# Queries, keys and score maxima as float16 pairs with a power-of-two scale, in a two-layer encoder of gated mixing and attention

## The chip, the core and the metric

The kernel runs on one core of a Trainium2 chip. Its engines work side by side, each through its own queue of instructions in order: TensorE (PE in the profile; its weight loads are PEld), VectorE (DVE), ScalarE (ACT), GpSimd (POOL) and SyncE (SP), which here issues all the transfers. TensorE writes to the eight banks of PSUM; everything else lies in SBUF or, in between, in DRAM. The metric is the device time of one execution in microseconds (us), lower is better.

## The reference

The input x is 2048 tokens by 1024 channels. Each of two layers does:

```python
h    = rmsnorm(x, pre_g[l])
proj = h @ w_in[l]                       # 1024 -> 2816 columns
u_a, v_a, g_a, q, k, v, g_b = split(proj)
y_a  = gmlp_group(u_a, v_a, ...) * silu(g_a)
y_b  = gqa_axial_attention(q, k, v, q_norm_g[l], k_norm_g[l], tables) * silu(g_b)
x    = x + rmsnorm(concat(y_a, y_b) @ w_out[l], post_g[l])
```

and the attention, with 8 query heads on 2 key heads of 64 channels, all tokens seeing all tokens:

```python
q = rope(rmsnorm(q, qn_g)); k = rope(rmsnorm(k, kn_g))
sc = einsum('bqkgd,bskd->bkgqs', qblk, k) * 64 ** -0.5
p  = softmax(sc)
o  = einsum('bkgqs,bskd->bqkgd', p, v)
```

Each head of q and k is normalised over its 64 channels and multiplied by a gain vector (`q_norm_g`, `k_norm_g`); in the inputs here these gains are about 8.

## The kernel before, in words

**Number format.** Products run on TensorE in a 32-bit format of reduced precision (F32R in the code, f32 in the profile). To keep accuracy, an operand is split in a high part (the value rounded to F32R) and a low part (the rest), and a product is made of two or three products of parts. Probabilities and values are pairs of float16.

**A layer has two stages.** In the projection stage (0 to 629 us and 1390 to 2019 us of the profile) the tokens go through in four groups of 512 (`GRP`), two at a time. `hT` holds the normalised, transposed tokens of a group, and every column block of `w_in` is loaded, split (`split_w`, lines 252 and 253) and multiplied. A list of small delayed jobs (`Background`, `bg.add(delay, f)`) is worked off between the products, two at most per `tick`: transposes, splits and stores go in there. With them, towards the end of the stage, goes the search for score maxima of the first eight units (`before`, called from `run`).

**Keys.** `do_kv` takes the projected keys of a group through `norm_rope` (lines 333 to 348) and writes, for each tile of 128 tokens and both key heads, a tile `kk` with three parts side by side: the high part (line 371, ScalarE), a second copy of it (372, ScalarE), and the low part (373, GpSimd). The delayed job `trans` transposes high and copy together, and the low part alone, four transposes a tile; line 380 (ScalarE) copies the first to `k_st`, whose 128 partitions hold the high part twice, and line 382 (VectorE) the other to the lower 64 partitions of `k_lo`. Row 64 of `k_lo` is a row of ones, written by a transfer from `ones1` once a layer (line 1167).

**Queries.** `do_q` does the same with a group's queries; its `trans` transposes first, then splits: line 397 (ScalarE) makes the high part `fh`, line 398 (VectorE) the low part `fl`, and four transfers put them into the DRAM tensor `q_d`.

**Attention.** A unit is one query block of 512 with one head: 32 units a layer, each with 16 key tiles. A unit needs a maximum for each query: `load_qm` brings its queries (high and low, 128 partitions) to `q_m`, 16 steps `max_step` multiply them with 512 keys at a time (`pmax`) and reduce on VectorE (`mx`), `max_row` negates, and `stack_max` transposes, adds the constant EXP_SHIFT on ScalarE (line 683) and stores the row into `m_d`. `load_q` brings `q_st` (high and low) and `q2` (the high part, and the maximum's row as row 64).

The order in the main loop of `attend` is written by hand: `PE`, `ACT`, `DVE` and `POOL` are engines wrapped so that their instructions keep program order, and in the profile all of these have line 84. For key tile k it issues: the two products `sp` (high keys with high and low queries; low keys and the row of ones with high queries and maxima), two exponentials from `sp`, one to the float16 `p_hi` (`p_parts<-sp`) and one to the 32-bit `p_f`, and a subtraction that makes the low part `p_lo`, on GpSimd or, for 15 tiles in 100, on VectorE. Then come jobs due at this step (`at`), a share of the output projection (`pout`, from the list `fill`), and the product of values with `p_hi` of three tiles ago (`LAG`). At every eighth tile a batch follows: the products of `p_lo` of eight tiles and the sums, 64 products with 32 columns of weights each (`po`, `sums`). `finish` divides by the sums and gates. Seven PSUM banks are shared by `sp`, `pmax`, `po`, `pout` and the small tiles.

**Memory.** `big` is a pool of seven buffers of 16 KB a partition for `hT`, `k_st`, `k_lo`, `v_st` and the split `w_out` (`wo`). `fp` has ten buffers of 2 KB for the small tiles.

**Gains.** `gains` loads both gain vectors, once in order and once with their halves swapped, and multiplies that of the queries by 64 ** -0.5 (line 198, VectorE). `rope_rows` multiplies the rotary table by them on GpSimd (line 325).

Of the kernel before, what the change touches and what calls it, by code (L numbers as in the profile page):

```python
# [19 lines left out]
P = 128  # L20
# [4 lines left out]
NH = 8  # L25
# [13 lines left out]
def encoder(ctx: ExitStack, tc, x, w_in, w_out, pre_g, post_g, ln_a_g, ln_a_b,  # L39
# [10 lines left out]
    big = ctx.enter_context(tc.tile_pool(name="big", bufs=7))  # L50
# [8 lines left out]
    def big_t(shape, name):  # L59
        return big.tile(shape, F32R, name=name, tag="big")  # L60
# [114 lines left out]
    class Project:  # L175
# [184 lines left out]
        def do_kv(self, g, banks):  # L360
# [6 lines left out]
            for i, kr in enumerate(krs):  # L367
                for j in range(2):
                    t = g * TPG + 2 * i + j
# [5 lines left out]
                    def trans(t=t, kk=kk):  # L375
# [4 lines left out]
                        nc.scalar.copy(k_st[:, :, t * P:(t + 1) * P],  # L380
                                       pk[:, 0:2 * P].rearrange("p (k s) -> p k s", k=NKV))
                        nc.vector.tensor_copy(k_lo[0:HD, :, t * P:(t + 1) * P],
                                              pk[0:HD, 2 * P:4 * P].rearrange("p (k s) -> p k s", k=NKV))
                    bg.add(KK_DELAY + 2 * (2 * i + j), trans)

        def do_q(self, g, banks, b):
            qrs = self.norm_rope([ps.rearrange("p (t h d) -> p t h d", t=2, d=HD) for ps in banks], 4,
                                 self.rope_rows(g, self.gain_q))
            for i, qr in enumerate(qrs):
                def trans(i=i, qr=qr):  # L390
# [7 lines left out]
                    nc.vector.tensor_tensor(lo, ps, hi.bitcast(F32), ALU.subtract)  # L398
                    for a, part in enumerate((hi, lo)):
                        for h in range(2):  # L400
                            dst = q_d[g][4 * b + h:4 * b + 4:2, a, :, i * 2 * P:(i + 1) * 2 * P]
                            nc.sync.dma_start(dst.rearrange("k d t -> d k t"),
                                              part.bitcast(F32)[h * HD:(h + 1) * HD])
# [212 lines left out]
    def attend(l, kv, nxt):  # L616
# [31 lines left out]
        def load_qm(u):  # L648
            qb, h = units[u]
            s = state[u]  # L650
            s.qm = f_t("q_m", dt=F32R)
            nc.sync.dma_start(s.qm.bitcast(F32), q_d[qb][h].rearrange("a d t -> (a d) t"))
            s.mx = small.tile([P, TPG, NG], F32, name="mx", bufs=3)

        def load_q(u):
            qb, h = units[u]
            s = state[u]
            s.qs = f_t("q_st", dt=F32R)
            nc.sync.dma_start(s.qs.bitcast(F32), q_d[qb][h].rearrange("a d t -> (a d) t"))
            s.q2 = f_t("q2", dt=F32R)  # L660
            nc.sync.dma_start(s.q2.bitcast(F32)[0:HD], q_d[qb][h, 0])
            nc.sync.dma_start(s.q2.bitcast(F32)[HD:HD + 1], m_d[qb][h:h + 1])
# [14 lines left out]
        def stack_max(u, pe, act):  # L677
# [4 lines left out]
            rows = small.tile([TPG, P], F32R, name="m_rows")  # L682
            act.activation(rows, ps[0:TPG, 0:P], AF.Copy, bias=EXP_SHIFT)
            nc.sync.dma_start(m_d[qb][h].rearrange("(t p) -> t p", p=P), rows.bitcast(F32))
# [388 lines left out]
        for k in range(end + 4):  # L1073
            if k < total:
# [9 lines left out]
                ACT.activation(p_hi(k), sp, AF.Exp)  # L1084
                ACT.activation(p_f(k), sp, AF.Exp)
# [76 lines left out]
    for l in range(DEPTH):  # L1162
        kv = [big_t([P, NKV, S], "k_st"), big_t([P, NKV, S], "k_lo")]
# [3 lines left out]
        nc.sync.dma_start(kv[1].bitcast(F32)[HD:HD + 1].rearrange("p k (n i) -> p (k n) i", i=P),  # L1167
                          ones1.unsqueeze(1).broadcast_to([1, NKV * S // P, P]))
# [44 lines left out]
```

## Time and profile before

| | us |
|---|---|
| median of 3 runs | 2810.36 (2807.75 to 2815.12) |
| the profiled execution | 2813.78 |
| its span | 2812.0 |
| projection stage of layer 1 and 2 | 628.9, 628.8 |
| attention stage of layer 1 and 2 | 761.0, 756.8 |
| mean granted TensorE clock | 0.993 |

The stages are bounded here by the first `sp` product or exponential and the last one. Busy time is the union of an engine's instructions; on TensorE and ScalarE an instruction's recorded time overlaps that of the next, so that the pace of a chain of instructions is read from the starts, and the time of one is longer than its step. A row of the groups reads: line, engine, operation, output<-inputs, shapes, count, busy us, mean ns of one, idle us of the engine just before, and what ended that idleness. A row of the windows reads: stretch, its length, then busy us and count for PE, PEld, DVE, ACT and POOL, the granted clock, the share of the transfer engines and GB/s. A row of the chain reads: start, length, engine and tile.

### The profile page before, as it was taken

How to read it: one execution, taken by the hardware profiler on the slowest of the kernel's cores; microseconds unless marked ns; L12 is line 12 of the kernel's file. 1: busy time of each engine (PE TensorE's matmuls, PEld its weight loads, DVE VectorE, ACT ScalarE, POOL GpSimd, SP SyncE). 2: the span in 40 equal slices, each digit the busy share in tenths (PEclk: the TensorE clock that was granted, in tenths of full speed). 3: DMA queues.
4: the chain of work that ended last, by engine and by line, in shares of the span. 5: the costliest groups of instructions: out<-in, count | busy, mean ns of one | idle time of the engine just before them, and what ended most of it. 6: DMA issues, size and time to landing. Idle time of an engine off the chain costs nothing.

```text
span 2812.0 us, 49354 instructions
## 1 busy us (share of the span) xinstructions
PE 2738.1 (97%) x18294; PEld 2067.2 (74%) x18294; DVE 1894.9 (67%) x3976; ACT 1583.3 (56%) x3295; POOL 1300.1 (46%) x1112
## 2 busy tenths in 40 slices
PE   7999999999999999999999999999999999999997
PEld 7998899885556666566699989998755666666665
DVE  7863788876666666666497639798766555656654
ACT  5322432228887777777642225322478877777774
POOL 1210121018776676666532111200377766767665
PEclk9999999999999999999999999999999999999999
DMA  4533433422222232232345343342322232221323
GB/s 134 165 110 108 137 108 90 124 90 97 85 85 89 94 91 97 87 100 89 139 151 151 122 128 121 102 124 91 112 68 94 78 100 71 83 92 59 115 71 127
DMA packets 276563, 293.71 MB, mean 104 GB/s; under 512 B 20450, under 2 KB 214306, under 8 KB 276324
## 3 DMA queue, kind: packets, MB, share of 16 engines
q1 hardware_dynamic: 276324, 290.57, 33.1%
q8 instruction: 145, 2.38, 0.3%
q14 instruction: 94, 0.77, 0.1%
HBM read 197.02 MB, written 93.45 MB: 103 GB/s over the span
## 4 chain that ended last, share of the span: by engine, by line
PE 79%; DVE 12%; ACT 4%; issue 2%; DMA 1%; POOL 1%; SPq 0%; DVEq 0%; POOLq 0%; ACTq 0%
PE pp L84 25%; PE sp L84 16%; PE pout L84 12%; PE po L84 12%; PE pmax L84 7%; PE sums L84 4%; PE pt L84 2%; DVE fc L346 2%; DVE w_lo L253 2%; ACT p_parts L84 1%; ACT p_f L84 1%; DMA w_raw<-in_w_in_dram 1%; DVE mx L670 1%; DVE o_t L84 1%; DVE fb L435 1%
## 5 line engine op out<-in xcount | busy, mean ns | idle before, releaser
L84 POOL TENSOR_TENSOR p_parts<-p_f,p_parts 128x512 f16<-128x512 f32 x872 | 1038.7, 1207 | 438.9 <-ACT p_f L84 256.7
L84 ACT ACTIVATE p_parts<-sp 128x512 f16<-128x512 f32 x1024 | 627.6, 613 | 334.5 <-PE sp L84 323.1
L84 DVE TENSOR_REDUCE mx<-pmax 128x1 f32<-128x512 f32 x768 | 515.0, 683 | 314.2 <-PE pmax L84 312.3
L84 PE MATMUL po<-p_parts,v_st 128*32 128x512 f16 (+1 forms) x3072 | 638.9, 383 | 0.0
L84 ACT ACTIVATE p_f<-sp 128x512 f32<-128x512 f32 x1024 | 629.3, 615 | 0.0
L84 PE MATMUL sp<-q_st,k_st 128*128 128x512 f32 x1024 | 578.7, 565 | 4.5 <-DVE mx L84 3.5
L84 PE MATMUL pp<-w_hi,hT 128*128 128x256 f32 x3584 | 494.8, 287 | 15.6 <-DVE hT L293 8.1
L84 PE MATMUL pout<-wo,y_t 128*128 128x512 f32 x1488 | 494.2, 397 | 0.0
L84 PEld LDWEIGHTS pp<-w_hi,hT 128*128 128x128 f32 x3584 | 461.1, 194 | 21.9 <-DVE hT L293 8.7
L84 PEld LDWEIGHTS <-v_st 128*32 128x32 f16 (+1 forms) x3072 | 193.0, 96 | 328.6 <-issue 287.4
L84 PE MATMUL pmax<-k_st,q_m 128*128 128x512 f32 x1024 | 409.7, 402 | 5.3 <-DVE mx L84 2.6
L84 PE MATMUL sp<-q,k_lo 65*128 65x512 f32 x1024 | 403.3, 394 | 0.0
L84 PEld LDWEIGHTS pout<-wo,y_t 128*128 128x128 f32 x1488 | 280.3, 189 | 60.8 <-DVE mx L84 1.7
L455 POOL TENSOR_TENSOR fl<-fa,fh 128x512 fp32r<-128x512 f32 x32 | 42.1, 1315 | 516.8 <-ACT fh L454 445.2
L84 PE MATMUL pp<-w_lo,hT 128*128 128x256 f32 x1792 | 262.4, 289 | 2.4 <-DVE w_lo L253 2.2
L84 PE MATMUL pp<-hT,w_hi 128*128 128x512 f32 x1024 | 257.8, 390 | 0.0
L84 PEld LDWEIGHTS sp<-q_st,k_st 128*128 128x128 f32 x1024 | 202.8, 198 | 65.2 <-issue 42.5
L84 PEld LDWEIGHTS pp<-w_lo,hT 128*128 128x128 f32 x1792 | 237.3, 194 | 6.6 <-DVE w_lo L253 4.8
L84 PE MATMUL sums<-p_parts,one_h 128*32 128x512 f16 x2048 | 241.8, 379 | 0.0
L252 ACT ACTIVATE w_hi<-w_raw,g_pre 128x256 fp32r<-128x256 f32 x352 | 151.8, 500 | 153.7 <-DMA w_raw<-in_w_in_dram 108.9
L84 PEld LDWEIGHTS pmax<-k_st,q_m 128*128 128x128 f32 x1024 | 193.4, 189 | 56.7 <-DVE mx L84 4.5
L84 PEld LDWEIGHTS pp<-hT,w_hi 128*128 128x128 f32 x1024 | 191.7, 188 | 39.7
(153 smaller groups left out, 3085.1 us busy)
## 6 DMA issues: line engine op xcount, KB each, us to landing
w_raw<-in_w_in_dram SPq DMA_DIRECT2D x28, 1024.0 KB
y_t<-y_d SPq DMA_DIRECT2D x56, 512.0 KB
w_raw<-in_w_in_dram SPq DMA_DIRECT2D x32, 512.0 KB
q_m<-q_d SPq DMA_DIRECT2D x64, 256.0 KB
q_st<-q_d SPq DMA_DIRECT2D x64, 256.0 KB
x_t<-in_x_dram SPq DMA_DIRECT2D x16, 512.0 KB
q_d<-fh SPq DMA_DIRECT2D x64, 128.0 KB
q_d<-fl SPq DMA_DIRECT2D x64, 128.0 KB
```

The costliest lines, as they stand in the source:

```text
L84: return tc.keep_in_program_order(call(*args, **kw))
L252: nc.scalar.activation(hi[:, d], raw[:, d], AF.Copy, scale=g)
L253: nc.vector.scalar_tensor_tensor(lo[:, d], raw[:, d], g, hi.bitcast(F32)[:, d], ALU.mult, ALU.subtract)
L346: nc.vector.tensor_tensor(t2[:, :, :, lo:lo + 16], qn[:, :, :, hi:hi + 16], tbi[:, :, 1:2, lo:lo + 16].broadcast_to([P, 2, n, 16]), ALU.mult)
L435: nc.vector.scalar_tensor_tensor(s.zt[r, c, :], pz[r, h * P:(h + 1) * P], self.lng[r, c:c + 1], self.zbias[r, c, :], ALU.mult, ALU.add)
L455: nc.gpsimd.tensor_tensor(lo, th, hi.bitcast(F32), ALU.subtract)
L670: dve.tensor_reduce(s.mx[:, j, c:c + 1], ps, AX.X, ALU.max)
```

## The change

Queries, keys and maxima are kept as float16 and multiplied as float16. So that float16 has the range, the gain vectors are first divided by the power of two in their largest entry; the product of both powers and 64 ** -0.5 is kept as `unit`, one number per partition, and the exponentials apply it as their scale. The constant EXP_SHIFT goes from the maxima's row to the exponentials' bias, also one number per partition (`shift`). The keys are no longer split ahead of their transposes: one ScalarE copy writes each key twice, two transposes a tile bring both copies to PSUM, ScalarE rounds them to float16 in `k_st`, and VectorE subtracts that from PSUM to get `k_lo`. Both lie in one tile `k_t` of 16 KB, and `big` has six buffers. The row of ones is a VectorE memset.

```diff
-    big = ctx.enter_context(tc.tile_pool(name="big", bufs=7))
+    big = ctx.enter_context(tc.tile_pool(name="big", bufs=6))
...
+    shift = const.tile([P, 1], F32, name="shift")
+    nc.vector.memset(shift, EXP_SHIFT)
...
-    q_d = [dram.tile([NH, 2, HD, GRP], F32, name=f"q_d{g}") for g in range(NG)]
-    m_d = [dram.tile([NH, GRP], F32, name=f"m_d{g}") for g in range(NG)]
+    q_d = [dram.tile([NH, 2, HD, GRP], F16, name=f"q_d{g}") for g in range(NG)]
+    m_d = [dram.tile([NH, GRP], F16, name=f"m_d{g}") for g in range(NG)]
...
-            nc.vector.tensor_scalar_mul(self.gain_q, self.gain_q, HD ** -0.5)
+            top = small.tile([P, 2, 2], F32, name="g_top")
+            e = small.tile([P, 2], F32, name="g_exp")
+            inv = small.tile([P, 2], F32, name="g_inv")
+            for i, gain in enumerate((self.gain_q, self.gain_k)):
+                nc.vector.tensor_reduce(top[:, i, 0:1], gain[:, 0], AX.X, ALU.max)
+                nc.vector.tensor_reduce(top[:, i, 1:2], gain[:, 0], AX.X, ALU.min, negate=True)
+            nc.vector.tensor_tensor(e, top[:, :, 0], top[:, :, 1], ALU.max)
+            ei = e.bitcast(I32)
+            nc.vector.tensor_scalar(ei, ei, EXP_BITS, None, ALU.bitwise_and)
+            nc.vector.tensor_scalar(ei, ei, float(97 << 23), float(157 << 23), ALU.max, ALU.min)
+            nc.vector.tensor_scalar(inv.bitcast(I32), ei, -1.0, float(254 << 23), ALU.mult, ALU.add)
+            for i, gain in enumerate((self.gain_q, self.gain_k)):
+                nc.vector.tensor_scalar(gain, gain, inv[:, i:i + 1], None, ALU.mult)
+            self.unit = lay.tile([P, 1], F32, name="unit", bufs=2)
+            nc.vector.tensor_scalar(self.unit, e[:, 0:1], e[:, 1:2], HD ** -0.5, ALU.mult, ALU.mult)
...
-                    kk = f_t("kk", 3 * NKV * HD).rearrange("p (k a d) -> p k a d", k=NKV, a=3)
-                    nc.scalar.copy(kk[:, :, 0, :].bitcast(F32R), kr[:, j])
-                    nc.scalar.copy(kk[:, :, 1, :], kk[:, :, 0, :])
-                    nc.gpsimd.tensor_tensor(kk[:, :, 2, :], kr[:, j], kk[:, :, 0, :], ALU.subtract)
+                    nc.scalar.copy(kk[:, NKV * j:NKV * (j + 1)], kr[:, j].unsqueeze(2).broadcast_to([P, NKV, 2, HD]))
...
-                            PE.transpose(pk[:, k * P:(k + 1) * P], kk[:, k, 0:2, :], ident)
-                            PE.transpose(pk[0:HD, (2 + k) * P:(3 + k) * P], kk[:, k, 2, :], ident)
...
+                            PE.transpose(pk[:, k * P:(k + 1) * P], kk[:, NKV * j + k], ident)
+                        pk = pk[:, 0:NKV * P].rearrange("p (k s) -> p k s", k=NKV)
+                        tt = slice(t * P, (t + 1) * P)
+                        nc.scalar.copy(k_st[:, :, tt], pk)
+                        nc.vector.tensor_tensor(k_lo[0:HD, :, tt], pk[0:HD], k_st[0:HD, :, tt], ALU.subtract)
...
-                    hi = f_t("fh", dt=F32R).rearrange("p (k t) -> p k t", k=2)
-                    lo = f_t("fl", dt=F32R).rearrange("p (k t) -> p k t", k=2)
+                    hi = f_t("fh", dt=F16).rearrange("p (k t) -> p k t", k=2)
+                    lo = f_t("fl", dt=F16).rearrange("p (k t) -> p k t", k=2)
...
-            s.qm = f_t("q_m", dt=F32R)
+            s.qm = f_t("q_m", dt=F16)
...
-            s.qs = f_t("q_st", dt=F32R)
+            s.qs = f_t("q_st", dt=F16)
...
-            s.q2 = f_t("q2", dt=F32R)
+            s.q2 = f_t("q2", dt=F16)
...
-            rows = small.tile([TPG, P], F32R, name="m_rows")
-            act.activation(rows, ps[0:TPG, 0:P], AF.Copy, bias=EXP_SHIFT)
+            rows = small.tile([TPG, P], F16, name="m_rows")
+            act.copy(rows, ps[0:TPG, 0:P])
...
-                ACT.activation(p_hi(k), sp, AF.Exp)
-                ACT.activation(p_f(k), sp, AF.Exp)
+                ACT.activation(p_hi(k), sp, AF.Exp, bias=shift, scale=layers[l].unit)
+                ACT.activation(p_f(k), sp, AF.Exp, bias=shift, scale=layers[l].unit)
...
-        kv = [big_t([P, NKV, S], "k_st"), big_t([P, NKV, S], "k_lo")]
+        k_t = big_t([P, 2, NKV, S], "k_t", F16)
+        kv = [k_t[:, 0], k_t[:, 1]]
...
-        nc.sync.dma_start(kv[1].bitcast(F32)[HD:HD + 1].rearrange("p k (n i) -> p (k n) i", i=P),
-                          ones1.unsqueeze(1).broadcast_to([1, NKV * S // P, P]))
+        nc.vector.memset(kv[1][HD:HD + 1], 1.0)
```

The number of `sp` and `pmax` products, of exponentials, of maxima and of transfers of queries stays the same; the bytes of those transfers halve.

More of the change, by code (lines that the diff above doesn't have):

```diff
@@ L57, in encoder, with big_t @@
     dram = ctx.enter_context(tc.tile_pool(name="dram", bufs=1, space=DRAM))
-    def big_t(shape, name):
-        return big.tile(shape, F32R, name=name, tag="big")
+    def big_t(shape, name, dt=F32R):
+        return big.tile(shape, dt, name=name, tag="big")
     def w_t(shape, name, dt=F32R):
@@ L367, in do_kv, with trans @@
             for i, kr in enumerate(krs):
+                kk = f_t("kk").rearrange("p (n a d) -> p n a d", a=2, d=HD)
                 for j in range(2):
-                    t = g * TPG + 2 * i + j
-                    kk = f_t("kk", 3 * NKV * HD).rearrange("p (k a d) -> p k a d", k=NKV, a=3)
-                    nc.scalar.copy(kk[:, :, 0, :].bitcast(F32R), kr[:, j])
-                    nc.scalar.copy(kk[:, :, 1, :], kk[:, :, 0, :])
-                    nc.gpsimd.tensor_tensor(kk[:, :, 2, :], kr[:, j], kk[:, :, 0, :], ALU.subtract)
-                    def trans(t=t, kk=kk):
+                    nc.scalar.copy(kk[:, NKV * j:NKV * (j + 1)], kr[:, j].unsqueeze(2).broadcast_to([P, NKV, 2, HD]))
+                    def trans(t=g * TPG + 2 * i + j, j=j, kk=kk):
                         pk = ps_t("pt")
                         for k in range(NKV):
-                            PE.transpose(pk[:, k * P:(k + 1) * P], kk[:, k, 0:2, :], ident)
-                            PE.transpose(pk[0:HD, (2 + k) * P:(3 + k) * P], kk[:, k, 2, :], ident)
[L380 to L383, printed above, removed]
+                            PE.transpose(pk[:, k * P:(k + 1) * P], kk[:, NKV * j + k], ident)
[3 more added lines that the diff above has]
+                        nc.vector.tensor_tensor(k_lo[0:HD, :, tt], pk[0:HD], k_st[0:HD, :, tt], ALU.subtract)
                     bg.add(KK_DELAY + 2 * (2 * i + j), trans)
@@ L402, in trans @@
                             nc.sync.dma_start(dst.rearrange("k d t -> d k t"),
-                                              part.bitcast(F32)[h * HD:(h + 1) * HD])
+                                              part[h * HD:(h + 1) * HD])
                 bg.add(Q_DELAY + 2 * i, trans)
@@ L681, in stack_max @@
             pe.transpose(ps[0:TPG, 0:P], s.m, ident)
-            rows = small.tile([TPG, P], F32R, name="m_rows")
-            act.activation(rows, ps[0:TPG, 0:P], AF.Copy, bias=EXP_SHIFT)
-            nc.sync.dma_start(m_d[qb][h].rearrange("(t p) -> t p", p=P), rows.bitcast(F32))
+            rows = small.tile([TPG, P], F16, name="m_rows")
+            act.copy(rows, ps[0:TPG, 0:P])
+            nc.sync.dma_start(m_d[qb][h].rearrange("(t p) -> t p", p=P), rows)
         def finish(u, k):
```

10 lines of the change are left out of this document (5 added, 5 removed).

## Prediction

> **What bounds the kernel now.** I read the page first (busy shares), then the windows of both attention stages in quarters of eight units (a unit is one head and one block of 512 queries: 16 key tiles, 32 exponentials), then the chain of waits and ScalarE's timeline inside a quarter, then the groups by shape for prices.
>
> ```profile
> span 2812.0 us, 49354 instructions
> PE 2738.1 (97%) x18294; PEld 2067.2 (74%) x18294; DVE 1894.9 (67%) x3976; ACT 1583.3 (56%) x3295; POOL 1300.1 (46%) x1112
> ```
>
> TensorE's 97% is modelled busy time, but it points the right way. ScalarE's 56% is a mean over two kinds of stage. Here are the eight quarters (length, then PE, PEld, DVE, ACT and POOL busy), and the last line is the sum of the same query for the tile `sp` alone, so its ACT is the 2048 exponentials:
>
> ```profile
> 628.88:801.76 172.88, 170.34 (x1131) 101.08 (x1130) 107.27 (x166) 144.37 (x290) 133.82 (x112) 1.00 0.29 93
> 801.76:994.96 193.20, 189.28 (x1258) 117.86 (x1257) 124.47 (x232) 148.80 (x302) 135.18 (x113) 1.00 0.28 88
> 994.96:1194.02 199.06, 196.17 (x1279) 121.98 (x1277) 134.99 (x253) 151.40 (x308) 137.12 (x115) 0.99 0.29 93
> 1194.02:1390.02 196.00, 195.94 (x1292) 124.25 (x1292) 111.95 (x205) 148.43 (x295) 133.87 (x114) 1.00 0.30 97
> 2018.71:2191.82 173.11, 170.12 (x1131) 101.08 (x1130) 107.00 (x166) 144.42 (x290) 133.78 (x112) 1.00 0.29 93
> 2191.82:2383.16 191.34, 189.05 (x1258) 117.89 (x1257) 114.90 (x202) 145.46 (x290) 134.43 (x113) 1.00 0.26 80
> 2383.16:2579.64 196.48, 194.07 (x1279) 121.09 (x1277) 122.25 (x213) 147.16 (x292) 136.42 (x115) 1.00 0.27 84
> 2579.64:2775.70 196.06, 196.00 (x1292) 124.26 (x1292) 108.61 (x195) 147.54 (x291) 134.00 (x114) 1.00 0.29 94
> sum 1518.13, PE 1500.96 PEld 929.48 DVE 931.44 ACT 1177.56 POOL 1078.63; mean PE 187.62 PEld 116.19 DVE 116.43 ACT 147.20 POOL 134.83
> ...
> sum 1518.13, PE 810.40 PEld 381.62 ACT 1080.64; mean PE 101.30 PEld 47.70 ACT 135.08
> ```
>
> The reader is to see two things. TensorE fills every quarter, and attention is 1518 of 2812 us. ScalarE stands at 147 of 190 us, so it has some 40 us of air in each quarter, least (28) in the first of each layer. ScalarE's work beside the exponentials is (1177.56 - 1080.64)/8 = 12.1 us a quarter. Next, the chain of waits around a steady tile and behind a batch of `p_lo` products:
>
> ```profile
> 702.34 0.23 PE pout L84
> 702.58 0.23 PE po L84
> 702.81 0.46 PE sp L84 x2
> 703.27 0.23 PE pmax L84
> ...
> 704.35 0.22 PE sums L84 x4
> ...
> 705.65 0.22 PE sums L84 x4
> ...
> 639.44 0.67 PE sp L84 x2
> ```
>
> The four 128-column products from 702.34 to 703.27 take 0.2325 us each, 32-bit (`sp`, `pout`) and float16 (`po`) alike; a group of four 32-column float16 products takes 0.217 (six groups from 704.35 to 705.65). The last row is from the first tiles of the layer: the two `sp` products behind a batch take 0.67 instead of 0.46, as their weight load no longer hides. Last, ScalarE at the start of attention, the one place where it is the bound:
>
> ```profile
> 629.84 0.60 ACT L84 ACTIVATE p_parts<-sp 128x512 f16<-128x512 f32 x1
> 638.90 0.85 ACT L84 ACTIVATE p_f<-sp 128x512 f32<-128x512 f32 x1
> 640.14 0.60 ACT L84 ACTIVATE p_parts<-sp 128x512 f16<-128x512 f32 x1 [0.39 <-PE sp L84]
> ```
>
> These are the first and the last of twenty in a row, and the next one: 19 steps in 9.06 us, 0.477 us each, though one alone lasts 0.60. Then TensorE's batch leaves ScalarE without scores for 0.39 us.
>
> **Part 1: scale and bias of the exponentials.** They had constants; now both are read from a [128,1] operand, 2048 times. The first row below is today's exponential; none with such an operand is in the trace, so the others are the nearest.
>
> ```profile
> L84 ACT ACTIVATE p_parts<-sp 128x512 f16<-128x512 f32 x1024 | 627.6, 613 | 334.5 <-PE sp L84 323.1
> L498 ACT ACTIVATE v_st<-v_st,v_exp 128x512 f16<-128x512 f32 x8 | 5.3, 711 | 0.0
> L422 ACT CAST fh<-fv 128x512 fp32r<-128x512 f32 x32 | 19.0, 618 | 37.9 <-DVE fv L416 33.3 <-POOL fl L423 4.7
> L134 DVE TENSOR_SCALAR rs_x<-rs_m 128x1 int32<-128x1 int32 x24 | 3.6, 148 | 0.2
> L137 DVE TENSOR_SCALAR rs_x<-rs_t,rs_x 128x1 f32<-128x1 f32 x72 | 13.6, 209 | 0.5
> L136 DVE TENSOR_SCALAR rs_t<-rs_x,rs_m 128x1 f32<-128x1 f32 x72 | 17.9, 268 | 0.7
> ```
>
> On ScalarE one operand (the scale of line 498) costs 711 - 618 = 93 ns on the same 128x512. For a second one there is only VectorE: none, one and two operands are 148, 209 and 268 ns, +61 and +59, so the second is as dear as the first. Bounds: 0 (hidden in the overlap; a gain is excluded, as nothing is left out) to 186 ns. I take 186, since both rows add up. An exponential then takes 0.477 + 0.186 = 0.663 us and a quarter's 256 take 169.7; with the other 12.1 us ScalarE needs **181.8 us a quarter**, where it had 122.1 + 12.1. The air is gone.
>
> The Trainium skill ("ScalarE: Activation LUTs", section What ACT_TABLE_LOAD costs) speaks against this part too: each [128,1] pointer operand adds about 93 ns. For one operand the trace agrees (93); for two no run here shows it.
>
> **Part 2: float16 queries and keys on TensorE.** Per quarter 256 `sp` and 96 `pmax` products change type (in the code 24 of a layer's 32 units have their 16 maximum steps here, the other 8 in the projection stage: 768 and 256 in all). Bounds: no gain, as the float16 `po` takes 0.23 too, to 16 ns each (0.2325 against 0.217, the two readings of the chain). I take 12 ns: 352 x 0.012 = 4.2 us. Behind each of 16 batches the weight load that lies open shrinks:
>
> ```profile
> L84 PEld LDWEIGHTS sp<-q_st,k_st 128*128 128x128 f32 x1024 | 202.8, 198 | 65.2 <-issue 42.5 <-ACT p_f L84 9.7 <-DVE mx L84 5.6
> L84 PEld LDWEIGHTS <-v_st 128*128 128x128 f16 x1024 | 98.0, 96 | 273.6 <-issue 272.5 <-DVE mx L84 0.7
> ```
>
> 198 - 96 = 0.1 us, 1.6 us. TensorE's need drops by **5.8 us a quarter** (bounds 0 to 7.2).
>
> The Trainium skill ("TensorE: Matmul & The Clock Gate", section Wait — 56ns, not 53.3ns?) gives 215.7 ns for 512 columns at full clock. By it the 12 would be 16 ns and the sum some 8 us lower; the groups of four agree (0.217), `po` in the chain (0.23) does not.
>
> **Part 3: which is later now, quarter by quarter.** First quarters: TensorE's 170.2 - 5.8 = 164.4 lies under ScalarE's 181.8, so ScalarE sets the pace. It loses something at each of 16 batches: 0.39 us as above, or less, because longer exponentials leave more of them queued when a batch begins. I take 0.3: 181.8 + 4.8 = 186.6 against 172.9 and 173.1, **+27.2 us** for both layers. Other quarters: TensorE's six busy times add to 1160.5, less 6 x 5.8 = 1125.7, or 187.6 a quarter; ScalarE needs 181.8. So near to each other, neither hides the other: units with much output projection wait on TensorE, the others on ScalarE. Today these 48 units wait 1172.1 - 1160.5 = 11.6 us, 0.24 each, with ScalarE far ahead. To that I add the full 0.39 us at two batches, as here no queue is built up: 1.02 us a unit, 49.0 us. 1125.7 + 49.0 = 1174.7 against 1172.1, **+2.6 us**. So TensorE's 35 us are eaten by the coupling. Bounds: 0.24 a unit (-34.8) to 2 a unit (+49.6).
>
> **Part 4: projection stages.**
>
> ```profile
> L84 PE MATMUL pt<-ident,kk 128*64 128x128 f32 x64 | 15.7, 272 | 0.0
> 1424.36 0.60 PE L84 MATMUL pt<-ident,x_h 128*128 128x128 f32 x4
> L474 DVE TENSOR_REDUCE v_top<-v_st 128x1 f32<-128x2048 f32 x2 | 4.5, 2270 | 0.0
> 5.89 0.21 DVE L133 TENSOR_SCALAR rs_m<-ss_x 128x1 f32<-128x1 f32 x1 [4.87 <-ACT sq L278]
> 1394.82 0.69 DVE L84 TENSOR_TENSOR o_t<-pout,o_t 128x512 f32<-128x512 f32 x1 [10.29 <-PE pout L84]
> ```
>
> The 64 transposes of the low key half go: four in a row take 0.60 with 0.27 for the last, so 0.11 each, -7.0 us. The 256 `pmax` of these stages give 256 x 0.012 = -3.1 us. The ones row becomes a VectorE memset of 4096 elements: by the reduction's 2270 ns for 2048, about 4.5 us, twice. It has no early reader, and VectorE has holes of 4.87 and 10.29 us where it can go; behind it on VectorE would wait the first `rs_x` chain or the layer's `hT` halves, so bounds 0 to 9; I take 1. `gains` gets some 13 small VectorE steps a layer at about 0.2 us (the 209 ns row), ahead of the rotary tables: 5.2 us, half of it seen, +2.6. The low keys now wait for the high half's copy, in the same two engines and order; one POOL subtraction and a ScalarE copy per tile go, off the path. The halved DMAs (SP's queue, issues unchanged in number) were hidden behind delays of several tiles: nothing. The pool has one buffer less and holds one tile less per layer; the next layer's second `hT` then follows the last `po` instead of the last `sp`, and it is written behind that anyway: nothing. Sum **-6 us**.
>
> **The sum.** 27.2 + 2.6 - 6 = +24 us (23.8). The profiled execution took 2813.78 us (span 2812.0), so 2838; it lies 3.4 above the median of the runs, 2810.36, and on that the forecast is **2834 us**.
>
> **Rivals.**
> A. The operands are read in the shade of the exponential before, or one at most shows. At 0.570 us each ScalarE needs 158 us a quarter and TensorE stays the bound: 8 x 5.8 + 6 = 52 us less, 2758. For it: steps overlap by 0.12 us already (0.60 against 0.477). Against: the VectorE rows add up. Chance 0.15.
> B. The other side, by queueing: the score banks let TensorE run so far ahead that batches cost ScalarE nothing. It decides if two finished scores are queued at each batch. First quarters 181.8 (+17.6), others -34.8, projection -6: 23 less, 2787. Against it: 0.39 us was lost with a queue full. Chance 0.17.
> C. A chain takes over. A batch needs `p_lo` of three tiles ago, so scores, two exponentials (1.33) and a POOL subtraction:
>
> ```profile
> L84 POOL TENSOR_TENSOR p_parts<-p_f,p_parts 128x512 f16<-128x512 f32 x872 | 1038.7, 1207 | 438.9 <-ACT p_f L84 256.7 <-PE sp L84 93.9 <-PE pmax L84 62.4
> ```
>
> That is 1.33 + 1.21 = 2.5 us, beside 3.8 for TensorE's three tiles (187.6/128 us each, less a batch's eight groups of 0.217 over eight tiles). Once ScalarE is over 1.3 us behind, each of 128 batches waits, up to 1.21 - 0.39 = 0.8 us more than I have: up to 102 us; I price it at half, 2885. Chance 0.13.
> D. The float16 products are no faster, so the change doesn't do what it says. The six quarters get 1160.5 + 49.0 (+37.4), and with 27.2 and -3 that is 2872. Chance 0.10.
>
> **The numbers.** My forecast has 0.45. The range goes from 2775 (B and part of A) to 2890 (C's middle). About 0.3% (8.4 us) is what a measurement can tell from no change. Faster: A, nearly all of B: 0.29. Same: the low end of the forecast and B's high end: 0.11. Slower: 0.60.
>
> **What would show it.** The group of exponentials should read about 800 ns instead of 613, the first quarters be longer by 10 to 18 us with ScalarE named in the chain, the projection stages shorter by a few us. ACT's idle time before `p_parts` (334.5 us, 323.1 of it for `sp`) should shrink below 100. If exponentials stay under 720 ns the forecast is wrong (A); if `p_parts` on POOL appears ahead of the batches in the chain, C; if `sp` pairs still take 0.46, D.

## The result, and the profile after

The changed kernel takes 2877.96 us (median of 4 runs, 2876.95 to 2881.4); the kernel before took 2809.06 us beside it (2806.72 to 2815.12). The ratio is 1.0244, 95% interval [1.0225, 1.0263]: slower by 69 us, where the forecast had slower by 24. The profiled execution took 2878.58 us, its span 2876.8.

First the page of the changed kernel: span, busy times, the chain that ended last, the two groups of exponentials.

```profile
span 2876.8 us, 48821 instructions
...
PE 2718.5 (94%) x18230; PEld 1783.9 (62%) x18230; DVE 1897.5 (66%) x3999; ACT 1897.8 (66%) x3263; POOL 1274.7 (44%) x1080
...
PE 56%; ACT 24%; DVE 14%; issue 2%; DMA 1%; POOL 0%; SPq 0%; DVEq 0%; ACTq 0%; POOLq 0%
...
L84 ACT ACTIVATE p_parts<-sp,shift,unit 128x512 f16<-128x512 f32 x1024 | 828.7, 809 | 68.6 <-PE sp L84 65.6
L84 ACT ACTIVATE p_f<-sp,shift,unit 128x512 f32<-128x512 f32 x1024 | 831.0, 812 | 0.0
```

The same line of the chain in the page of before:

```profile
PE 79%; DVE 12%; ACT 4%; issue 2%; DMA 1%; POOL 1%; SPq 0%; DVEq 0%; POOLq 0%; ACTq 0%
```

The reader is to see ScalarE step into the chain, from 4% to 24%, with exponentials of 809 ns instead of 613, and its idle time ahead of `p_parts` fall from 334.5 to 68.6 us. It is the second bound now. TensorE's 94% still looks full, but records overlap in it; the windows tell more. These are the changed kernel's eight attention quarters (columns as before), and as the last line the sum of the same query for `sp` alone:

```profile
635.85:829.18 193.33, 172.57 (x1134) 72.43 (x1133) 105.36 (x167) 187.08 (x289) 131.10 (x112) 0.98 0.22 71
829.18:1027.60 198.42, 188.21 (x1259) 87.42 (x1258) 125.45 (x232) 188.39 (x301) 133.51 (x113) 0.99 0.23 74
1027.60:1228.96 201.36, 192.19 (x1280) 89.47 (x1279) 130.83 (x253) 190.71 (x308) 134.76 (x114) 1.00 0.25 80
1228.96:1424.31 195.35, 192.15 (x1288) 94.56 (x1286) 110.70 (x205) 186.83 (x297) 134.61 (x113) 1.00 0.25 79
2062.39:2253.72 191.33, 170.91 (x1134) 71.96 (x1133) 105.79 (x167) 186.88 (x290) 131.15 (x112) 0.99 0.22 71
2253.72:2447.53 193.81, 185.92 (x1259) 87.10 (x1258) 114.81 (x202) 184.58 (x289) 132.72 (x113) 1.00 0.21 68
2447.53:2645.70 198.17, 191.20 (x1280) 89.65 (x1279) 118.93 (x213) 186.10 (x292) 134.04 (x114) 1.00 0.22 70
2645.70:2841.07 195.37, 192.15 (x1288) 94.59 (x1286) 107.60 (x195) 185.67 (x293) 134.83 (x113) 1.00 0.24 77
sum 1567.14, PE 1485.31 PEld 687.17 DVE 919.46 ACT 1496.24 POOL 1066.73; mean PE 185.66 PEld 85.90 DVE 114.93 ACT 187.03 POOL 133.34
...
sum 1567.14, PE 611.62 ACT 1407.64; mean PE 76.45 ACT 175.95
```

ScalarE is busy for 187 us of every quarter, and in the first ones, where TensorE has the least to do (172.57 and 170.91), it sets the length. Attention takes 1567.1 us instead of 1518.1. The span's 64.8 us split so: first quarters +20.5 and +18.2, the other six +10.4 together (1172.1 to 1182.5), the two projection stages +7.0 and +9.3, the tail -0.6. Last, ScalarE at the start of attention:

```profile
635.85 0.77 ACT L84 ACTIVATE p_parts<-sp,shift,unit 128x512 f16<-128x512 f32 x1
636.52 0.77 ACT L84 ACTIVATE p_f<-sp,shift,unit 128x512 f32<-128x512 f32 x1
...
651.08 0.92 ACT L84 ACTIVATE p_f<-sp,shift,unit 128x512 f32<-128x512 f32 x1
651.74 0.92 ACT L84 ACTIVATE p_parts<-sp,shift,unit 128x512 f16<-128x512 f32 x1
```

From the first to the last row lie 24 steps in 15.89 us, 0.662 us each. It was 0.477.

### The profile page after: what moved, and what is told of

Read it like the earlier page. It is cut to its first block, busy times and chain, and to the rows that moved or that the text cites. A ratio compares the mean times of both kernels' runs of the same rounds, so it can differ in the third digit from the quotient of the medians.

```text
span 2876.8 us, 48821 instructions
## 1 busy us (share of the span) xinstructions
PE 2718.5 (94%) x18230; PEld 1783.9 (62%) x18230; DVE 1897.5 (66%) x3999; ACT 1897.8 (66%) x3263; POOL 1274.7 (44%) x1080
## 4 chain that ended last, share of the span: by engine, by line
PE 56%; ACT 24%; DVE 14%; issue 2%; DMA 1%; POOL 0%; SPq 0%; DVEq 0%; ACTq 0%; POOLq 0%
PE pp L84 24%; ACT p_f L84 11%; ACT p_parts L84 10%; PE sp L84 8%; PE pout L84 8%; PE po L84 7%; PE pmax L84 4%; PE sums L84 3%; DVE w_lo L269 2%; DVE fc L362 2%; PE pt L84 2%; DVE mx L682 1%; DVE fb L447 1%; ACT o_pair L84 1%; DVE o_t L84 1%
## 5 line engine op out<-in xcount | busy, mean ns | idle before, releaser
L84 POOL TENSOR_TENSOR p_parts<-p_f,p_parts 128x512 f16<-128x512 f32 x872 | 1027.5, 1180 | 500.1 <-ACT p_f L84 368.8
L84 ACT ACTIVATE p_parts<-sp,shift,unit 128x512 f16<-128x512 f32 x1024 | 828.7, 809 | 68.6 <-PE sp L84 65.6
L84 ACT ACTIVATE p_f<-sp,shift,unit 128x512 f32<-128x512 f32 x1024 | 831.0, 812 | 0.0
L84 PE MATMUL pout<-wo,y_t 128*128 128x512 f32 x1488 | 658.1, 506 | 6.7 <-ACT p_f L84 5.5
L84 PE MATMUL pp<-w_hi,hT 128*128 128x256 f32 x3584 | 502.3, 289 | 16.3 <-DVE hT L309 9.9
L84 PE MATMUL pmax<-k_t,q_m 128*128 128x512 f16 x1024 | 390.1, 382 | 36.3 <-ACT p_f L84 24.0
L84 PE MATMUL sp<-q_st,k_t 128*128 128x512 f16 x1024 | 391.0, 382 | 30.2 <-ACT p_f L84 17.8
L84 PE MATMUL sp<-q,k_t 65*128 65x512 f16 x1024 | 391.8, 383 | 0.0
L84 PEld LDWEIGHTS <-k_t 128*128 128x128 f16 (+1 forms) x2048 | 190.8, 99 | 226.5 <-issue 118.0
L84 PE MATMUL pp<-hT,w_hi 128*128 128x512 f32 x1024 | 271.7, 413 | 0.0
L84 PEld LDWEIGHTS pp<-w_lo,hT 128*128 128x128 f32 x1792 | 235.5, 193 | 12.1 <-DVE w_lo L269 10.5
L84 DVE TENSOR_TENSOR p_parts<-p_f,p_parts 128x512 f16<-128x512 f32 x152 | 111.3, 732 | 169.7 <-ACT p_f L84 169.5
```

Source lines behind the costliest of these rows:

```text
L84: return tc.keep_in_program_order(call(*args, **kw))
```

## The experiments

My theory after the result: the two operands on the exponentials cost all that was lost in attention and more, the float16 products gain about what Part 2 said, and the projection stages got longer for a reason that the forecast did not have. The rivals were the forecast's: the chain through GpSimd's subtraction (C), float16 products that are no faster (D), and, for the rest, batches that starve ScalarE. The table has all twelve kernels. Ratios are to the kernel before on the same chip; stages are sums over both layers, from the traces; a step is the start-to-start time of two exponentials in a row while scores are queued, so that ScalarE does not wait between them.

| kernel | median us | ratio, 95% interval | projection | attention | step |
|---|---|---|---|---|---|
| before | 2809 to 2811 | 1 | 1257.7 | 1518.1 | 0.477 |
| changed | 2877.96 | 1.0244 [1.0225, 1.0263] | 1273.9 | 1567.1 | 0.662 |
| e1 constants | 2786.85 | 0.9915 [0.9898, 0.9931] | 1275.0 | 1473.6 | 0.478 |
| e2 scale operand alone | 2816.75 | 1.002 [1.001, 1.0029] | 1275.6 | 1503.7 | 0.570 |
| e3 ones on GpSimd | 2873.06 | 1.0222 [1.0207, 1.0237] | 1269.8 | 1561.9 | 0.663 |
| e4 before, with operands | 2892.75 | 1.0295 [1.0279, 1.031] | 1252.5 | 1601.4 | 0.663 |
| e5 plain float16 | 2781.73 | 0.9895 [0.988, 0.991] | 1268.9 | 1474.4 | 0.478 |
| e6 e5, old key split | 2779.71 | 0.9888 [0.9872, 0.9905] | 1269.3 | 1474.7 | 0.478 |
| e7 batches of 4 | 2895.22 | 1.0303 [1.0288, 1.0318] | 1279.7 | 1582.9 | 0.663 |
| e8 `p_lo` a tile later | 2891.75 | 1.0289 [1.0274, 1.0305] | 1278.1 | 1579.2 | 0.663 |
| e9 e5, seven big buffers | 2790.48 | 0.9925 [0.9908, 0.9943] | 1280.2 | 1475.2 | 0.477 |
| e10 e2, six banks | 2889.89 | 1.0289 [1.0271, 1.0307] | 1282.6 | 1567.8 | 0.570 |
| e11 e5, six banks | 2848.47 | 1.0137 [1.0121, 1.0153] | 1272.6 | 1535.3 | 0.477 |
| e12 e5, maxima in pairs | 2789.2 | 0.993 [0.9917, 0.9944] | 1276.9 | 1476.2 | 0.477 |

### The operands: e1, e2, e4

**e1**, the changed kernel with constants in the exponentials:

```diff
-  ACT.activation(p_hi(k), sp, AF.Exp, bias=shift, scale=layers[l].unit)
-  ACT.activation(p_f(k), sp, AF.Exp, bias=shift, scale=layers[l].unit)
+  ACT.activation(p_hi(k), sp, AF.Exp, bias=EXP_SHIFT, scale=8.0)
+  ACT.activation(p_f(k), sp, AF.Exp, bias=EXP_SHIFT, scale=8.0)
```

> The changed kernel with scale 8.0 and bias EXP_SHIFT as constants in both exponentials (8.0 is what unit comes to for these inputs), all else as changed. Theory 1 (the two operands are what fills ScalarE in attention): the exponential's step falls from 0.662 to about 0.48 us, TensorE is the bound again with about 6 us a quarter less work than before the change, and the time is about 2775 us: attention near 1470 us, the projection stages still about 16 us longer than before the change. Theory 2 (changes between float16 and 32-bit products, or the coupling by PSUM banks, cost as much as the operands): above 2830 us.

It took 2786.85, 12 us over the 2775 of theory 1 and far below the 2830 of theory 2: 91 us less than the changed kernel and 24 less than before, so the operands alone make the change slower, and without them it is a gain. Its attention is 44.5 us under that of before, 5.6 a quarter: that is what the float16 products are worth. Its group of exponentials, with the idle time ahead of it back at 294.5 us:

```profile
L84 ACT ACTIVATE p_parts<-sp 128x512 f16<-128x512 f32 x1024 | 628.8, 614 | 294.5 <-PE sp L84 287.8
```

**e2** keeps the scale operand and makes only the bias a constant (`bias=EXP_SHIFT, scale=layers[l].unit`).

> The changed kernel with the bias as a constant and the scale still read from its operand. Theory 1 with each operand at 93 ns: step about 0.57 us, ScalarE needs about 159 us a quarter, below TensorE's, so nearly all is regained: 2780 to 2795 us. If the two operands are read together and either alone costs 186 ns: about 2878, unchanged.

It took 2816.75, 30 us more than e1, well above what was expected. Its group of exponentials:

```profile
L84 ACT ACTIVATE p_parts<-sp,unit 128x512 f16<-128x512 f32 x1024 | 731.0, 714 | 169.5 <-PE sp L84 160.2
```

One operand adds 100 ns to the record (614 to 714) and 92 to the step (0.478 to 0.570), the second another 95 and 92. The step is the steadier of the two, as a record grows while scores are queued (from 0.77 to 0.92 us in the changed kernel's rows above). The Trainium skill ("ScalarE: Activation LUTs", section What ACT_TABLE_LOAD costs) says about 93 ns for each, which speaks for Part 1 and not against it; the trace agrees for both. Neither is hidden behind the exponential before. The step of 0.570 makes 146 us a quarter, 160 with the other work of 13.9 (the mean of the eight, its steps added up by kind), while these quarters last 177 to 195. So ScalarE was not the bound, and a longer exponential cost 3.8 us a quarter all the same: 17 of the 30 us in the two first quarters, where the two engines' needs lie nearest, and 13 in the other six. Of this more below.

**e4** is the kernel before with both operands at their neutral values, 1.0 and 0.0, and nothing else.

```diff
-  ACT.activation(p_hi(k), sp, AF.Exp)
-  ACT.activation(p_f(k), sp, AF.Exp)
+  ACT.activation(p_hi(k), sp, AF.Exp, bias=shift, scale=unit)
+  ACT.activation(p_f(k), sp, AF.Exp, bias=shift, scale=unit)
```

> The kernel before, with a scale of 1.0 and a bias of 0.0 read from [128,1] operands in both exponentials; nothing else of the change. Theory 1: step 0.66 us; ScalarE needs the same 183 us a quarter as in the changed kernel and TensorE a little more than there, so attention grows by 50 to 70 us, to 2860 to 2880 us, while the projection stages stay as before. Theory 2: below 2840 us.

It took 2892.75, a ratio of 1.0295, above the 2860 to 2880 expected: the operands cost 83 us of attention by themselves, more than the whole change does. With them float16 still gains, 34 us of attention (1601.4 to 1567.1); without them, 44.5. So the gain shrinks by 10 us once ScalarE is the bound.

### The rest of the change: e3, e5, e6

**e3** moves the row of ones to GpSimd (`nc.gpsimd.memset` for `nc.vector.memset`).

> The changed kernel with the row of ones set on GpSimd instead of VectorE. If the 3.47 us memset lies on the way to the first products of each layer, as its place ahead of hT in both layers suggests: 4 to 7 us less, about 2872 us. If it is hidden: 2878 us, unchanged.

It took 2873.06, 4.9 us less by the medians; the two intervals overlap, so this is near the limit of what can be told apart. The memset's place on VectorE in the changed kernel, layer 2:

```profile
1452.19 3.47 DVE L1180 MEMSET k_t<- 1x4096 f16 x1 [0.91 <-issue]
1455.69 4.87 DVE L84 TENSOR_TENSOR hT<-pt,hT 128x512 fp32r<-128x512 f32 x8
```

It runs for 3.47 us directly ahead of the eight `hT` instructions that TensorE's first products need.

**e5** drops the power-of-two scaling too: the gains are multiplied by 64 ** -0.5 as before, the exponentials have constants, the ones are on GpSimd. Nothing then guards the range of float16, which holds for gains of about 8.

```diff
-  top = small.tile([P, 2, 2], F32, name="g_top")
...
-  nc.vector.tensor_scalar(self.unit, e[:, 0:1], e[:, 1:2], HD ** -0.5, ALU.mult, ALU.mult)
+  nc.vector.tensor_scalar_mul(self.gain_q, self.gain_q, HD ** -0.5)
...
+  ACT.activation(p_hi(k), sp, AF.Exp, bias=EXP_SHIFT)
+  ACT.activation(p_f(k), sp, AF.Exp, bias=EXP_SHIFT)
...
+  nc.gpsimd.memset(kv[1][HD:HD + 1], 1.0)
```

> Float16 queries, keys and maxima without the power-of-two scaling: the queries' gain is multiplied by 64 ** -0.5 as before the change, the exponentials have scale 1 and the bias EXP_SHIFT as constants, and the ones are set on GpSimd. It computes the same for gains of this size, without the guard for the range of float16. Against e1_const (2786.85): the ones give 5 us (as measured by themselves). If the 13 small VectorE steps of gains hold up the start of each layer, the projection stages get shorter by another 5 to 12 us, to about 2772. If they are hidden: about 2782.

It took 2781.73, 1.05% under before: with e6 the best version here. Against e1 with the memset's 4.9 us taken off (2782), the small steps of `gains` cost nothing that can be seen.

**e6** is e5 with the keys split ahead of their transposes as in the kernel before (its low part then misses what float16 rounds off beyond the 32-bit format).

> e5_plain with the keys split ahead of their transposes as before the change (two ScalarE copies, a GpSimd subtraction and four transposes a tile); the low part then misses what float16 rounds off beyond the 32-bit format. If the new order of the key split, where VectorE's subtraction stands behind ScalarE's copy, is what lengthened the projection stages: 5 to 10 us less than e5_plain. If the 64 transposes saved are all that counts: 4 to 8 us more.

2779.71: neither number. The order of the split makes no difference to the time, though it does to the work. The windows over both projection stages show how; here are their sums. The kernel before:

```profile
sum 1257.68, PE 1217.88 PEld 1123.62 DVE 940.19 ACT 399.25 POOL 207.39; mean PE 608.94 PEld 561.81 DVE 470.10 ACT 199.62 POOL 103.69
```

The changed kernel:

```profile
sum 1273.93, PE 1214.20 PEld 1082.90 DVE 954.69 ACT 394.83 POOL 193.08; mean PE 607.10 PEld 541.45 DVE 477.35 ACT 197.41 POOL 96.54
```

e5:

```profile
sum 1268.90, PE 1215.82 PEld 1085.21 DVE 944.50 ACT 395.81 POOL 199.81; mean PE 607.91 PEld 542.61 DVE 472.25 ACT 197.91 POOL 99.90
```

And e6:

```profile
sum 1269.30, PE 1223.32 PEld 1092.57 DVE 942.93 ACT 398.64 POOL 213.68; mean PE 611.66 PEld 546.28 DVE 471.46 ACT 199.32 POOL 106.84
```

Length less PE's busy time is what TensorE waited: 39.8, 59.7, 53.1 and 46.0 us. From e6 to e5 the missing transposes save 7.5 us of TensorE's work, and 7.1 come back as waits. Of TensorE's waits (us in all, times, longest) this one stands out in e5:

```profile
PE pt L84 <- DVE fc L348: 7.0, 4, 2.3
```

In e6 the nearest to it is:

```profile
PE pt L84 <- DVE fc L341: 2.8, 3, 1.7
```

### Batches and the chain through GpSimd: e7, e8

In the changed kernel ScalarE still waits after batches, at 1069.63 us for 1.28:

```profile
1069.63 0.78 ACT L84 ACTIVATE p_parts<-sp,shift,unit 128x512 f16<-128x512 f32 x1 [1.28 <-PE sp L84]
```

**e7** halves the batches (`BATCH = 4`), so that each stop is half as long.

> The changed kernel with batches of four tiles instead of eight (BATCH = 4): half as long, twice as many. ScalarE idles for 101 us in attention in the changed kernel, nearly all of it waiting for sp. If the long batch starves it: idle falls by 40 to 60 us and the time to 2825 to 2850 us, although TensorE pays 128 more changes of weights (0.2 us each). If PSUM banks or something else set it: 2870 to 2900 us.

2895.22, 17 us more. ScalarE's idle time before `p_parts` did not fall by 40 to 60 us; it is 80.3 us instead of 68.6. So the theory that long batches starve ScalarE falls.

**e8** lets each batch come a tile later (`LAG_LO = 4` for 3), which gives GpSimd's subtraction more time.

> The changed kernel with LAG_LO = 4, so that a batch uses p_lo of four tiles ago instead of three. If a batch waits for GpSimd's subtraction behind the late exponentials (rival C): 20 us or more less, below 2860. If not, and the trace shows no such wait: 2874 to 2882 us.

2891.75, 14 us more. If batches had waited for `p_lo` (rival C), it would have been less. GpSimd has 0% of the chain above, too. That it took longer was in neither expectation; a part goes with TensorE's granted clock (0.986 to 0.988 in its runs, 0.988 to 0.991 in the changed kernel's), the rest stays open.

### Run-ahead: e10, e11

Why did e2 lose 30 us with ScalarE below its bound? TensorE can only run ahead as far as there are PSUM banks, and a bank stays taken until its second exponential is done. **e10** is e2, and **e11** is e5, with one bank less:

```diff
-  return psum.tile([P, GRP], F32, name=name, tag="ps", bufs=7)
+  return psum.tile([P, GRP], F32, name=name, tag="ps", bufs=6)
```

> The changed kernel with only the scale read from an operand, and six PSUM banks instead of seven for the shared tiles (seven gave 2817, 30 over the version with constants, though ScalarE's need of 159 us a quarter lies well under TensorE's). Theory that the loss comes from how far TensorE can run ahead, which the banks set: one bank less makes the same kind of loss larger, 15 to 40 us more, 2832 to 2857, and it falls on the units with few output products. Rival, that the loss comes from the order of the instructions and not from the number of banks: 2817 within 5.

> The plain version (no power-of-two scaling and no guard of float16's range, constants, ones on GpSimd) with six PSUM banks instead of seven for the shared tiles; the control for the same with the scale operand. Theory of the banks: with exponentials of 613 ns a bank is held for less time and there is more room, so one bank less costs less here, 5 to 20 us, 2787 to 2802. Rival, that banks do not matter: 2782 within 5. If it loses more than the version with the operand does, the theory falls as well.

They took 2889.89 and 2848.47: one bank costs 73 us in e2 and 67 in e5 (64 and 61 of attention). Both are far above what either theory gave, so banks do matter, and much. But the difference between the two, 6 us, is about as large as the uncertainty of these ratios, so it is not shown that longer exponentials make the banks scarcer. Nor does e10's loss fall mainly on the units with few output products, as the theory had it: the two first quarters have 18 of its 64 us. These are the two largest waits of TensorE in the changed kernel, for `p_f`, which frees a bank:

```profile
PE pmax L84 <- ACT p_f L84: 24.0, 47, 1.7
PE sp L84 <- ACT p_f L84: 17.8, 46, 1.0
```

In e2 the same two:

```profile
PE pmax L84 <- ACT p_f L84: 7.4, 18, 1.5
...
PE sp L84 <- ACT p_f L84: 6.2, 18, 0.8
```

In the kernel before, the groups by shape give `pmax` 0.9 us behind `p_f` and `sp` 0.4. So the wait is there, it grows with the exponential's length, and with e2's 13.6 us it is under half of e2's 30.

### The projection stages: e9, e12

**e9** is e5 with the pool `big` back at seven buffers (`bufs=7`).

> The plain version (no power-of-two scaling and no guard of float16's range, constants in the exponentials, ones on GpSimd), with seven buffers in the pool big instead of six. Theory that the missing buffer is what lengthens the projection stages: both come back to at most 629 us (from 636.4 and 632.5), the attention quarters stay, total about 2771. Rival, that the buffer has nothing to do with it (the tile that is gone is not waited for): 2782 within 4, stages at 636 and 632.

2790.48, 9 us more instead of 11 less: the missing buffer is not the cause. Nothing in the kernel's text says why it got slower, but the traces say where. Of the 11.3 us by which the two stages are longer than in e5, 3.5 are waits of TensorE (56.6 us against 53.1). This one was 0.8 us in e5:

```profile
PE t L84 <- DVE m_neg L671: 7.7, 4, 3.1
```

The other 7.7 us are busy time (1223.56 against 1215.82) for the same instructions. That fits TensorE's granted clock, which in these stages is at half for 44 us here and for 27 in e5. One such interval stands right behind the longest wait for `m_neg`, which ends at 631.11:

```profile
631.60:634.90 3.30, 3.30 (x10) 2.53 (x9) 0.00 (x0) 0.36 (x2) 0.00 (x0) 0.50 0.12 36
```

**e12** tests another cause. In this stretch of the first projection stage one `pmax` comes between every four 32-bit products. TensorE's timeline in the kernel before:

```profile
548.32 0.39 PE L84 MATMUL pmax<-k_st,q_m 128*128 128x512 f32 x1
...
555.14 0.39 PE L84 MATMUL pmax<-k_st,q_m 128*128 128x512 f32 x1
```

The same in the changed kernel:

```profile
559.76 0.39 PE L84 MATMUL pmax<-k_t,q_m 128*128 128x512 f16 x1
559.79 1.28 PE L84 MATMUL pp<-hT,w_hi 128*128 128x512 f32 x4
560.91 0.39 PE L84 MATMUL pmax<-k_t,q_m 128*128 128x512 f16 x1
...
565.55 0.39 PE L84 MATMUL pmax<-k_t,q_m 128*128 128x512 f16 x1
```

Before, six cycles of five products take 6.82 us, 1.137 each; after, five take 5.79, 1.158 each. The cycle with the float16 product is the longer one, by 21 ns. In e12 the maxima of these stages come two at a time:

```diff
-  bg.add(n0 + 4 + n, lambda u=u, n=n: max_step(u, n, PE, nc.vector))
+  bg.add(n0 + 4 + (n | 1), lambda u=u, n=n: max_step(u, n, PE, nc.vector))
```

> The plain version (no power-of-two scaling and no guard of float16's range, constants, ones on GpSimd; 2781.7), with the maxima products of the projection stages issued two at a time instead of one between every four 32-bit products. Theory that a float16 product among 32-bit ones pays for two changes of format: five products with one pmax take 1.158 us in the trace, where the all 32-bit kernel takes 1.137; ten with a pair should then take about 2.29 instead of 2.32, 128 pairs 3 to 5 us in all, 2777 to 2779. Rival, that the products do not care for their neighbours and the longer stages come from waits alone: ten take 2.32 and the time stays at 2782, or rises if VectorE's reductions now come in pairs and hold a bank.

TensorE's timeline in e12, in the same stage:

```profile
556.70 0.60 PE L84 MATMUL pmax<-k_t,q_m 128*128 128x512 f16 x2
556.95 2.19 PE L84 MATMUL pp<-hT,w_hi 128*128 128x512 f32 x8
558.99 0.61 PE L84 MATMUL pmax<-k_t,q_m 128*128 128x512 f16 x2
```

Ten products now take 2.29 us (558.99 - 556.70) instead of 2.32: the theory of the format changes holds to the number. The time, 2789.2, is nevertheless 7 us above e5, as the rival's last clause had it. TensorE waits 9.8 us for the queries' maxima ahead of their transposes, which is the second of its waits in e12:

```profile
PE t L84 <- DVE m_neg L671: 9.8, 4, 3.8
```

That VectorE's reductions in pairs make the maxima late is not shown by this, as e9 has nearly the same wait without pairs. And here, too, the clock is at half for 44 us of the two stages instead of 27. Each run's time multiplied by its granted clock is an estimate of the time at full clock; the means lie between 2760 and 2763 us for e1, e5, e6, e9 and e12. So most of the 5 to 9 us between these kernels goes with the clock, which falls behind waits of TensorE (see the last section).

## Why the prediction was right and where it was wrong

The direction was right, and so was the cause: two operands fill ScalarE, which becomes the second bound. The size was not: the span grew by 64.8 us, 41 more than the 23.8 of the forecast's sum. Part 4, the projection stages, has 22 of these with a wrong sign; Part 3 has 11.5 in the first quarters and 7.8 in the others, where the cost of stops between the two engines was taken too small.

**Part 1 was right.** 0.663 us was forecast for an exponential's step, 0.662 measured, and the second operand is as dear as the first. That excludes rival A: with one operand the step is 0.570, and two run at full price.

**Part 2 was right in its sum** (5.8 us a quarter, e1 gives 5.6), and that excludes rival D. Its reading of a flat 12 ns was not: from the ends of neighbouring products in the changed kernel's trace, float16 behind float16 takes 216 to 218 ns, float16 behind 32-bit 231, 32-bit behind float16 226 to 240. The gain sits in the pairs of equal format, and behind the batches, where the open step is 323 ns instead of 432. That the mean still came out near 12 ns, which was a choice between bounds of 0 and 16, is in part luck.

**Part 3, first quarters: mechanism right, size too small** (+27.2 forecast, +38.7 measured). ScalarE sets the pace, as said. Two terms were off. Its other work is 14.3 us in these quarters when its steps are added up by kind, not the 12.1 that came from a difference of two busy times, which are unions of overlapping records: 4.4 us for both layers. And ScalarE loses 9.7 and 7.7 us there to stops, counted by starts (the time from one start to the next beyond the step of the first), instead of 4.8 each: 7.8 us. (A step of 0.662 for 0.663 gives 0.5 back.) The forecast had read 0.39 us for a stop from the end of the last record; by the starts in its own rows (638.90 and 640.14), less the step of 0.477, ScalarE lost 0.76 us there.

**Part 3, other quarters: mechanism right, size a little small** (+2.6 against +10.4). The forecast said that TensorE's 35 us would be eaten by the coupling, at 1.02 us a unit. They were, and 8 more: (1182.5 - 1125.7)/48 = 1.18 a unit. e1, without the operands, takes 1137.0 us for these six quarters, which is the forecast's 1125.7 and 0.24 a unit; so the term that was too small is what the long exponentials add, 0.95 a unit instead of 0.78. Whether it comes at two batches a unit, as forecast, was not measured. That this coupling costs something even where ScalarE has room (e2) was not in the forecast, whose rival A had 52 us less at 0.570. e10 and e11 show that a bank less costs 61 to 64 us of attention; that e2's 30 us come by way of the banks is not shown, and their cause stays open.

**Part 4 was wrong, in its sign**: "Sum **-6 us**" (its terms add to -6.5) became +16.3. The transposes were right: -7.0 forecast, -7.5 of busy time measured between e6 and e5. But the step assumed that work taken from TensorE shortens the stage, and 7.1 came back as waits. For `pmax` it took -3.1; the float16 products gain nothing among 32-bit ones and lengthen the next, 256 x 21 ns = +5.4 if every one of them pays what the stretch above shows, and e6's busy time, which has no other change on TensorE, is also 5.4 above that of before (1223.32 - 1217.88). The memset was taken at 1 us within 0 to 9; e3 gives 4.9, near the limit of what can be told apart. The gains' 2.6 are not seen (the steps are eleven a layer, not 13). There remain 6.2 us of waits in e6 (46.0 - 39.8) that no experiment here explains; e9 shows that it is not the pool. With e4, whose projection code is that of before, the same stages take 1252.5 instead of 1257.7: TensorE's clock is at half there for 10 us, and for 27 in the kernel before. The changed kernel and e6 also have 27, so that the clock does not explain the 16.3 us; but single terms of 5 or 6 us in this account are near what one profiled execution can tell from another.

**The rivals.** Of what was to show the steps, three came: exponentials near 800 ns (809), ScalarE in the chain, its idle time under 100 us (68.6). The first quarters got longer by more than the 10 to 18 us named (20.5 and 18.2), and the projection stages did not get shorter. B is excluded, as batches do cost ScalarE time; C by e8 and the chain.

## What to carry to other kernels

A [128,1] operand on an activation is paid in full each time, so a factor that can go into a constant or be folded into data ahead of the loop should not ride on thousands of exponentials; here that choice turned a gain of 1% into a loss of 2.4%. An engine that is busy 160 of 188 us is not free: where two engines hand buffers to each other, a longer step of the second needs a price of its own, even below its bound (30 us in e2). The cost of a stop is read from starts, not from the ends of records. And work taken off the bounding engine counts only after one has asked, stage by stage, what its waits will be then.

## What the hardware showed that was not expected

Products of two formats on TensorE disturb each other: a 512-column product takes 227 ns in a row of 32-bit ones (`pp`) and 216 to 218 in a row of float16 ones, but a change of format costs enough that one float16 product among four 32-bit ones makes the five slower than five of 32 bits (1.158 against 1.137 us).

TensorE's granted clock fell to half after a wait of 1.73 us for a bank, in the changed kernel. The windows around it (stretch, length, busy times, clock):

```profile
760.00:766.00 6.00, 4.86 (x22) 2.00 (x21) 2.77 (x5) 5.58 (x11) 4.14 (x4) 1.00 0.59 192
766.50:770.00 3.50, 3.41 (x9) 1.26 (x9) 2.65 (x5) 3.50 (x7) 1.87 (x2) 0.52 0.11 31
770.00:775.00 5.00, 5.00 (x55) 2.27 (x54) 0.80 (x3) 3.62 (x6) 3.92 (x4) 0.99 0.00 2
```

TensorE's timeline there:

```profile
763.23 0.38 PE L84 MATMUL sp<-q,k_t 65*128 65x512 f16 x1
...
766.59 0.56 PE L84 MATMUL pmax<-k_t,q_m 128*128 128x512 f16 x1 [1.73 <-ACT p_f L84]
...
768.24 0.63 PE L84 MATMUL sp<-q,k_t 65*128 65x512 f16 x1
```

The same product lasts 0.63 us instead of 0.38 for some 3.5 us. The Trainium skill ("TensorE: Matmul & The Clock Gate", section A second HAM failure mode: psum-queue depth-cycling) describes a kernel that cycles through PSUM banks, in which TensorE's short idle times between groups of products come often enough that the clock swings between half and full. This place agrees in kind. The trace has ten such intervals of 3.4 or 6.8 us ahead of its tail, four of them in attention (one in the kernel before), and in the 3.4 us ahead of each TensorE was busy for 2.3 us or less. So a short wait can be paid a second time behind it. The runs of the changed kernel have a mean clock of 0.988 to 0.991, those of the kernel before 0.993 to 0.995; 0.4% of the time is some 11 us, an upper estimate of the clock's share in the 69; the forecast had no term for it.

The memset of 4096 float16 elements on one partition took 3.47 us on VectorE, where the forecast had estimated 4.5 from a reduction, and 3.50 on GpSimd.
